# Moving SSM loads to ScalarE's queue, state products beside output products, and the slots of the attention around the query norms

## The chip, the cores and the metric

The kernel runs on one core of a Trainium2 chip. Five engines matter: TensorE (PE, with its weight loads as PEld), VectorE (DVE), ScalarE (ACT), GpSimd (POOL) and SyncE (SP). Each runs its own instructions in program order and waits for the others by semaphores. DMAs are issued by SP or ACT, as instructions in that engine's stream. The metric is the device time of one execution in microseconds; the times below are medians of several executions.

## The reference

One layer of a hybrid decoder for 256 prompt tokens and 8 x 4 decode tokens, 288 columns in all, width 2048, in fp32:

```
x = x + 1/2 SwiGLU_1(rmsnorm(x))
u, q, k, v = split(rmsnorm(x) @ w_in)          # 1024 + 1024 + 256 + 256 columns
y_ssm  = S5(u): h_t = lam_bar * h_(t-1) + B_bar u_t (complex), y = gelu(Re(C h) + D u), then a GLU
y_attn = sliding window attention over 128 keys, 16 query heads on 4 key heads,
         q and k normed per head, ALiBi, one sink per head
x = x + concat(rmsnorm(y_ssm), rmsnorm(y_attn)) @ w_out
x = x + 1/2 SwiGLU_2(rmsnorm(x))
```

The key and value caches and the SSM states are outputs too. The S5 part has 64 groups of 16 channels with 64 complex states; the kernel treats it in 8 blocks j of 128 channels, with the scan over chunks of 4 tokens (T=4), so that the steps within a chunk are small matrix products with prepared matrices (ma into the state, mb out of it) and the steps between chunks a scan with a decay (d0) in a rotating frame (rot).

## The kernel before, in words

All weights stream through in 677 pieces of at most 128 x 1024 fp32. Every fp32 product is three products of rounded parts (mm3, lines L290, L291, L292: high x high, low x high, high x low). For each piece SP loads the raw tile (L116), ACT casts the high part wh (L124), VectorE subtracts the low part wl (L125), and TensorE makes 24 matmuls with it. Class Weights sets the order: `W.next()` begins a **slot**, one for each piece. It first splits the piece two slots ahead, issues the raw loads ahead, then runs the actions that were registered for this slot with `W.at(slot, f)`, and only then the slot's own 24 matmuls follow. `W.spread(slot, generator)` runs one step of a generator in each slot from there on. Nothing else sets the order: it is a list written out by hand, and each engine keeps it.

The mixer's slots are counted here from `base`: 0 and 1 key, 2 to 17 the eight SSM blocks (two slots each), 18 and 19 key, 20 to 23 value, 24 to 39 the eight query tiles i (two heads each; two tiles, a pair m, share one run of norms), 40 to 71 w_out.

An SSM block j starts from s = 7, 9, ... (base + 2j + 5). Its projection is stored to scratch memory (ssm_u_store, L761, ACT's queue) and read back in another layout as U, four DMAs (ssm_u_load, L767, SP's queue). ssm_load_a and ssm_load_r read ma and rot (L771, L775), ssm_load_b mb (L789), all on SP. ssm_state makes 32 small matmuls (L798) into a rotated sum (L804 to L807, VectorE), then one slot later the scan (L810 to L814), then cs (L818 on ACT, L820 on POOL, L821), then L823, L824 and ACT's copy fin (L825). ssm_out makes 48 matmuls from U, cs and mb (L833) and a gelu (L837). For every two blocks, ssm_y_store writes the result out in four DMAs (L843, ACT's queue), ssm_y_load reads it back as yn (L847, SP's queue), and ssm_glu multiplies it with the GLU weights (L856, L861) and splits it for w_out (L743). ssm_norm is the chain of an rsqrt over 288 columns (L230 to L246) that gives R_ssm, with which the w_out results are scaled (L1177).

In the attention, q_square squares a query tile (L1007, ACT, reading qn of L1171), sums adds the squares over each head (L1025, TensorE) and starts row_rsqrt, a chain of one VectorE instruction (L970) and twelve small ones on POOL (L973 to L976). scores makes the logits on TensorE (L1043), scales them with the query norm (L1049, ACT) and adds the bias (L1053, VectorE), and runs the softmax, whose last step (L1001) multiplies the probabilities lg by the inverse sum. probs_t transposes them (L1062, TensorE; L1063) and pv multiplies with the values (L1075). The decode tokens have their own path (sample).

The helpers `get` and `put` are a DMA issued by SP and by ACT. `tt`, `ts` and `stt` are VectorE's tensor_tensor, tensor_scalar and scalar_tensor_tensor.

Of the kernel before, what the change touches and what calls it, by code (L numbers as in the profile page):

```python
# [14 lines left out]
ALU = mybir.AluOpType  # L15
AX = mybir.AxisListType

P = 128
# [15 lines left out]
EPS = 1e-6  # L34
# [656 lines left out]
def mix(tc, nc, io, es, W, base, e):  # L691
    act, dve, pool_e, pe = nc.scalar, nc.vector, nc.gpsimd, nc.tensor
    tt, ts, stt = dve.tensor_tensor, dve.tensor_scalar, dve.scalar_tensor_tensor
    x, R, gains, ident, acc = e["x"], e["R"], e["gains"], e["ident"], e["acc"]
    tp, dr, pm, pa = (e[k] for k in ("tp", "dr", "pm", "pa"))
    proj, mm3 = e["proj"], e["mm3"]
    put, get = act.dma_start, nc.sync.dma_start
# [16 lines left out]
    R_ssm = mp.tile([P, N], F32, name="R_ssm")  # L714
# [7 lines left out]
    yd = [dr.tile([2 * P, N], F32, name="yd%d" % j) for j in range(4)]  # L722
# [27 lines left out]
    MA, MB, ROT, D0, U, CS, UE, YG, YN, GL = ({} for _ in range(10))  # L750
# [12 lines left out]
    def ssm_u_load(j):  # L763
        U[j] = sm.tile([P, 4, W1], F32, name="U", bufs=4)
        src = ud[j].rearrange("(q c) (j t) -> j c q t", q=4, j=T)
        for jr in range(T):
            get(U[j][32 * jr:32 * jr + 32], src[jr])  # L767

    def ssm_load_a(j):
        MA[j] = sa.tile([P, 2, 4, P], F32, name="ma", bufs=2)  # L770
# [20 lines left out]
    def ssm_state(j):  # L791
        ma, u, rot = MA.pop(j), U[j], ROT.pop(j)
        b = []
        for i in range(2):
            ps = aux()
            for q in range(4):
                for hh in HALVES:
                    pe.matmul(ps[hh, q * W1:(q + 1) * W1], ma[:, i, q, hh], u[:, q], start=True, stop=True)  # L798
            b.append(ps[:, :N].rearrange("p (q t) -> p q t", q=4))
        br, bi = b[0][:, :, NB:], b[1][:, :, NB:]  # L800
        co, si = rot[:, :, 0, :], rot[:, :, 1, :]
        z, w = (sa.tile([P, 2, 4, NCH], F32, name="r" + n, bufs=2) for n in "zw")
        q = slice(4 * j, 4 * j + 4)
        tt(z[:, 1], br, co, op=ALU.mult)  # L804
        tt(w[:, 1], bi, si, op=ALU.mult)
        tt(z[:, 0], bi, co, op=ALU.mult)
        tt(w[:, 0], br, si, op=ALU.mult)  # L807
        yield
        for i in range(2):
            tt(fin_s[:, i, q, :], b[i][:, :, :NB], fin_s[:, i, q, :], op=ALU.add)  # L810
        tt(z[:, 1], z[:, 1], w[:, 1], op=ALU.add)
        tt(z[:, 0], z[:, 0], w[:, 0], op=ALU.subtract)
        for i in range(2):
            dve.tensor_tensor_scan(flat(w[:, i]), flat(D0[j % 2]), flat(z[:, i]), 0.0, op0=ALU.mult, op1=ALU.add)  # L814
        yield
        cs = CS[j % 2]
        for i in range(2):
            act.copy(cs[:, i, :, :NB], e["h0"][:, 1 - i, q, :])  # L818
        both = [P, 2, 4, NCH]
        pool_e.tensor_tensor(z, w, si[:, None].to_broadcast(both), op=ALU.mult)  # L820
        tt(cs[:, :, :, NB + 1:], w, co[:, None].to_broadcast(both), op=ALU.mult)  # L821
        yield
        tt(cs[:, 1, :, NB + 1:], cs[:, 1, :, NB + 1:], z[:, 0], op=ALU.subtract)  # L823
        tt(cs[:, 0, :, NB + 1:], cs[:, 0, :, NB + 1:], z[:, 1], op=ALU.add)  # L824
        act.copy(fin[:, :, q], cs[:, :, :, W1])  # L825

    def ssm_out(j):
# [16 lines left out]

    def ssm_y_load(j):
        YN[j] = sm.tile([P, 2, N], F32, name="yn", bufs=2)
        get(YN[j], yd[j].rearrange("(a p) n -> p a n", a=2))  # L847

    def glu_load():
        GL[0] = sm.tile([P, 8, P], F32, name="gl")  # L850
# [2 lines left out]
    def ssm_glu(j):  # L853
        yn = YN[j // 2][:, j % 2]
        ps = aux()
        pe.matmul(ps[:, :N], GL[0][:, j], yn, start=True, stop=True)  # L856
        t = tp.tile([P, N], F32, name="s1")
        act.activation(t, ps[:, :N], AF.Tanh, scale=0.5)
        yield
        y2 = tp.tile([P, N], F32, name="s2")  # L860
        stt(y2, t, 1.0, yn, op0=ALU.add, op1=ALU.mult)  # L861
        yield
        yield from y_split(ys, y2, 48 + j, j == 0, dve if j == 7 else pool_e)
# [16 lines left out]
    for j in range(8):  # L880
        s = base + 2 * j + 5
        W.at(s, ssm_u_store, j)
        W.at(s + 1 if j > 1 else base + 1 + j, ssm_load_a, j)
        W.at(s + 1 if j > 1 else base + 2 + j, ssm_load_r, j)
        W.at(s + 2, ssm_u_load, j)
        W.at(s + 2, ssm_decay, j)
        W.spread(s + 4, ssm_state(j), True)
        W.at(s + 6, ssm_load_b, j)
        W.at(s + 9, ssm_out, j)
        if j % 2:  # L890
            W.at(s + 10, ssm_y_store, j // 2)
            W.at(s + 11, ssm_y_load, j // 2)
            W.spread(s + 13, ssm_glu(j - 1))
            W.spread(s + 14, ssm_glu(j))
    W.at(s + 8, state_done)
    W.at(s + 17, ssm_done)

    def ssm_norm():
        for n, _ in enumerate(e["norm"](e["ones"], acc, R_ssm, 1.0 / 1024, 4 * EPS)):
            if n % 2:  # L900
                yield

    W.spread(s + 19, ssm_norm())

    def tok(ap, blk):

# [73 lines left out]
    def softmax(lg, parts, sink, w):  # L980

        m = mp.tile([P, w], F32, name="sm_m", bufs=4)
        es_ = mp.tile([P, w], F32, name="sm_e", bufs=4)
        l = mp.tile([P, w], F32, name="sm_l", bufs=4)
        for a, (lo, hi) in enumerate(parts):
            dve.tensor_reduce(m[:, 2 * a:2 * a + 2], lg[:, :, lo:hi], axis=AX.X, op=ALU.max)
        tt(m, m, sink, op=ALU.max)
        tt(es_, sink, m, op=ALU.subtract)
        ts(m, m, -1.0, None, op0=ALU.mult)
        yield  # L990
        for a, (lo, hi) in enumerate(parts):
            for hb in range(2):
                c = 2 * a + hb
                act.activation(lg[:, hb, lo:hi], lg[:, hb, lo:hi], AF.Exp, bias=m[:, c:c + 1],  # L994
                               accum_out=l[:, c:c + 1])
        act.activation(es_, es_, AF.Exp)
        yield
        tt(l, l, es_, op=ALU.add)
        dve.reciprocal(l, l)
        for a, (lo, hi) in enumerate(parts):  # L1000
            pool_e.tensor_tensor(lg[:, :, lo:hi], lg[:, :, lo:hi],  # L1001
                                 l[:, 2 * a:2 * a + 2, None].to_broadcast([P, 2, hi - lo]), op=ALU.mult)

    def q_square(i):
        qb = QN[i]
# [11 lines left out]
    def sums(m):  # L1017

        ps = aux()
        cols = 8  # L1020
        for i in (2 * m, 2 * m + 1):
            for blk in range(2):
                c = 4 * (i % 2) + 2 * blk
                for hh in HALVES:
                    pe.matmul(ps[hh, c:c + 2], QN[i][1][:, 128 * blk:128 * blk + 128][:, hh],  # L1025
                              bones[:, 0:128:64], start=True, stop=True)
        if m % 2:
            cols = 10
            for hh in HALVES:
                pe.matmul(ps[hh, 8:10], QS[m // 2][1][:, hh], bones[:, 0:128:64], start=True, stop=True)  # L1030
        v = mp.tile([P, 10], F32, name="rq_v", bufs=2)[:, :cols]
        ts(v, ps[:, :cols], 1.0 / 64, EPS, op0=ALU.mult, op1=ALU.add)
        RQ[m] = row_rsqrt(v, cols)

    def scores(i):
        p, g = divmod(i, 4)
        qb, sq = QN.pop(i)
        rq = RQ[i // 2][:, 4 * (i % 2):4 * (i % 2) + 4]
        pss = [aux() for _ in range(2)]
        for a, (bq, bk) in enumerate(((0, 0), (1, 0), (1, 1))):  # L1040
            for hb in range(2):
                pp = slice(64 * hb, 64 * hb + 64)
                pe.matmul(pss[hb][:, 128 * a:128 * a + 128], qb[pp, 128 * bq:128 * bq + 128],  # L1043
                          tok(kG[pp, p], bk), start=True, stop=True)
        yield
        lg = L[i] = late["a"].tile([P, 2, 384], F32, name="lg", bufs=3)
        for hb in range(2):
            for blk, (lo, hi) in enumerate(((0, 128), (128, 384))):
                act.activation(lg[:, hb, lo:hi], pss[hb][:, lo:hi], AF.Copy,  # L1049
                               scale=rq[:, 2 * blk + hb:2 * blk + hb + 1])  # L1050
        yield
        for hb in range(2):
            stt(lg[:, hb], dist, -SLOPES[heads_of(i)[hb]], lg[:, hb], op0=ALU.mult, op1=ALU.add)  # L1053
        yield from softmax(lg, ((0, 128), (128, 384)), sinkp[:, 4 * i:4 * i + 4], 4)
# [92 lines left out]
                next(y, None)  # L1147
            yield

    S = [base + 2 * (12 + i) + 2 for i in range(8)]  # L1150
    for i, s in enumerate(S):
        W.at(s, q_square, i)
        W.at(s + 11, pv, i)
    for m in range(4):
        W.at(S[2 * m + 1] + 1, sums, m)
    for i in range(8):
        W.spread(S[i | 1] + 1 + i % 2, scores(i))
    for i, s in enumerate(S):
        W.at(s + 9, probs_t, i)
    for p in range(2):  # L1160
        s = base + 2 * (12 + 4 * p + 3) + 2
        W.at(s - 4, cache_k_load, p)
# [190 lines left out]
```

## Time and profile before

| what | value |
|---|---|
| median of 3 runs | 1874.78 us (1873.18 to 1879.98) |
| profiled execution | 1878.1 us, span 1876.2 us, mean granted clock 0.996 |
| TensorE weight loads, share of the span | 98% |
| weights and all else moved by DMA | 359.08 MB, mean 191 GB/s |
| DMA share in the mixer's SSM stage (800 to 850 us) | 0.87 |
| DMA share in the attention stage (950 to 1000 us) | 0.35 |

The mixer runs from about 800 to 1100 us of the span; before and behind it lie the two feed-forward parts. A wait is put down to the engine or DMA whose semaphore came last by the profile. The granted clock of TensorE (PEclk) is a share of its full speed. A DMA's time to landing counts from its issue to the arrival of its data.

### The profile page before, as it was taken

What the parts mean: (1) busy time and instruction counts of PE and PEld (TensorE: products, weight loads), DVE (VectorE), ACT (ScalarE), POOL (GpSimd) and SP (SyncE); (2) the same over time, 40 slices, a digit from 0 to 9 for tenths busy, and PEclk for the clock granted to TensorE, in tenths of its full rate; (3) what the DMA queues carried; (4) which work ended last, traced back from release to release, by engine and by line L of the source; (5) the groups of instructions that cost most, each with busy time, mean ns of one, the idle gap of its engine ahead of it and who ended that gap; (6) DMA issues with size and microseconds to landing.
All of it is one profiled execution on the core that took longest, in us unless ns stands there. A gap on an engine that the chain in (4) does not pass through costs nothing.

```text
span 1876.2 us, 38183 instructions
## 1 busy us (share of the span) xinstructions
PE 1857.0 (99%) x15620; PEld 1839.1 (98%) x15620; DVE 1207.7 (64%) x1857; ACT 853.6 (45%) x1347; POOL 269.0 (14%) x342
## 2 busy tenths in 40 slices
PE   9999999999999999999989999999999999999999
PEld 9999999999999999998988999999999999999999
DVE  6677667666667755688887885555555555555554
ACT  6443444444444444643566554433444334434433
POOL 3201011000100100212236640000000000000000
PEclk9999999999999999999999999999999999999999
DMA  7555656556655764788733455556555565556555
GB/s 277 197 181 163 219 181 214 190 166 230 212 192 162 232 213 147 238 293 292 232 120 135 157 176 185 179 161 188 187 179 168 174 196 180 163 169 207 180 161 160
DMA packets 122624, 359.08 MB, mean 191 GB/s; under 512 B 22064, under 2 KB 30256, under 8 KB 121264
## 3 DMA queue, kind: packets, MB, share of 16 engines
q1 hardware_dynamic: 114496, 340.48, 56.7%
q10 hardware_dynamic: 7952, 16.16, 2.5%
q8 instruction: 122, 2.00, 0.4%
q14 instruction: 54, 0.44, 0.1%
HBM read 338.40 MB, written 20.22 MB: 191 GB/s over the span
## 4 chain that ended last, share of the span: by engine, by line
PE 93%; DVE 3%; ACT 1%; DMA 1%; POOL 1%; issue 1%; SPq 0%; ACTq 0%; POOLq 0%; DVEq 0%
PE main L290 30%; PE main L292 30%; PE main L291 30%; DVE wl L125 1%; ACT wh L124 1%; PE main L833 1%; DMA ud<-t 0%; PE main L798 0%; PE main L623 0%; PE main L629 0%; ACT lg L994 0%; DMA ma<-mats 0%; DMA raw<-in_w_gu 0%; POOL x L1178 0%; POOL lg L1001 0%
## 5 line engine op out<-in xcount | busy, mean ns | idle before, releaser
L125 DVE TENSOR_TENSOR wl<-raw,wh 128x1024 fp32r<-128x1024 f32 (+2 forms) x677 | 754.1, 1114 | 445.0 <-ACT wh L124 443.1
L290 PE MATMUL main<-xh,wh 128*128 128x288 f32 x3136 | 904.9, 289 | 0.5 <-ACT xh L216 0.5
L292 PE MATMUL main<-xh,wl 128*128 128x288 f32 x3136 | 899.7, 287 | 0.7 <-DVE wl L125 0.6
L291 PE MATMUL main<-xl,wh 128*128 128x288 f32 x3136 | 899.4, 287 | 0.1
L124 ACT CAST wh<-raw 128x1024 fp32r<-128x1024 f32 (+2 forms) x677 | 637.9, 944 | 495.9 <-PE main L291 335.4
L290 PEld LDWEIGHTS main<-xh,wh 128*128 128x128 f32 x3136 | 594.6, 190 | 3.9 <-ACT xh L216 0.8
L292 PEld LDWEIGHTS main<-xh,wl 128*128 128x128 f32 x3136 | 594.5, 190 | 1.7 <-DVE wl L125 0.8
L291 PEld LDWEIGHTS main<-xl,wh 128*128 128x128 f32 x3136 | 594.7, 190 | 1.3 <-DVE xl L217 0.8
L290 PE MATMUL main<-hh,wh 128*128 128x288 f32 x1664 | 478.2, 287 | 0.3 <-ACT s L1079 0.3
L291 PE MATMUL main<-hl,wh 128*128 128x288 f32 x1664 | 476.3, 286 | 0.6 <-DVE hl L743 0.6
L292 PE MATMUL main<-hh,wl 128*128 128x288 f32 x1664 | 476.2, 286 | 0.0
L290 PEld LDWEIGHTS main<-hh,wh 128*128 128x128 f32 x1664 | 314.8, 189 | 1.2 <-ACT s L1079 0.8
L291 PEld LDWEIGHTS main<-hl,wh 128*128 128x128 f32 x1664 | 314.8, 189 | 1.0 <-DVE hl L743 0.8
L292 PEld LDWEIGHTS main<-hh,wl 128*128 128x128 f32 x1664 | 314.8, 189 | 0.2 <-DVE wl L125 0.2
L364 POOL TENSOR_TENSOR s<-s,R 128x288 f32<-128x288 f32 x88 | 70.6, 803 | 1139.5 <-ACT s L363 1139.5
L373 ACT CAST hh<-h 128x288 fp32r<-128x288 f32 x88 | 38.1, 433 | 222.5 <-DVE h L372 222.5
L363 ACT ACTIVATE s<-t 128x288 f32<-128x288 f32 x88 | 39.1, 445 | 219.5 <-DVE t L362 219.5
L394 DVE SCALAR_TENSOR_TENSOR x<-main,x 128x288 f32<-128x288 f32 x128 | 58.4, 457 | 39.7 <-PE main L292 39.3
L372 DVE TENSOR_TENSOR h<-main,s 128x288 f32<-128x288 f32 x88 | 40.1, 456 | 55.5 <-PE main L292 55.2
L362 DVE TENSOR_TENSOR t<-main,R 128x288 f32<-128x288 f32 x88 | 40.2, 456 | 44.9 <-PE main L292 44.6
L374 DVE TENSOR_TENSOR hl<-h,hh 128x288 fp32r<-128x288 f32 x88 | 40.4, 459 | 44.0 <-ACT hh L373 44.0
L226 POOL TENSOR_TENSOR acc<-acc,sq 128x288 f32<-128x288 f32 x45 | 45.3, 1006 | 46.0 <-ACT sq L222 45.1
(262 smaller groups left out, 835.8 us busy)
## 6 DMA issues: line engine op xcount, KB each, us to landing
raw<-in_w_gu SPq DMA_DIRECT2D x349, 512.0 KB, 4.1
raw<-in_w_dn SPq DMA_DIRECT2D x128, 384.0 KB, 3.2
raw<-in_w_dn SPq DMA_DIRECT2D x128, 320.0 KB, 3.2
raw<-in_w_in SPq DMA_DIRECT2D x40, 512.0 KB, 4.9
raw<-in_w_out SPq DMA_DIRECT2D x32, 512.0 KB, 3.5
mats<-stage ACTq DMA_DIRECT2D x8, 1536.0 KB, 7.1
mb<-mats SPq DMA_DIRECT2D x8, 768.0 KB, 8.2
ma<-mats SPq DMA_DIRECT2D x8, 512.0 KB, 5.4
```

The source lines that it names most:

```text
L124: self.nc.scalar.copy(wh[:, :n], t[:, :n])
L125: self.nc.vector.tensor_tensor(wl[:, :n], t[:, :n], wh[:, :n].bitcast(F32), op=ALU.subtract)
L226: eng.tensor_tensor(acc, acc, sq, op=ALU.add)
L290: pe.matmul(ps, wh[:, s], woven(rh[k]), start=first and a == 0, stop=False)
L291: pe.matmul(ps, wh[:, s], woven(rl[k]), start=False, stop=False)
L292: pe.matmul(ps, wl[:, s], woven(rh[k]), start=False, stop=last and a == n - 1)
L362: dve.tensor_tensor(t1, pg[:, :N], R, op=ALU.mult)
L363: act.activation(s1, t1, AF.Silu)
L364: pool_e.tensor_tensor(s2, s1, R, op=ALU.mult)
L372: dve.tensor_tensor(halved(h), evens(pu[:, :N]), evens(s2), op=ALU.mult)
L374: dve.tensor_tensor(hl, h, hh.bitcast(F32), op=ALU.subtract)
L394: dve.scalar_tensor_tensor(x[d], ps[:, :N], 0.5, x[d], op0=ALU.mult, op1=ALU.add)
```

## The change

In the SSM part, U is loaded in slot s+1 instead of s+2 and by ACT instead of SP; ma and rot in slot s instead of s+1 (both for j over 1 in the latter case); the state products run in slot s+3 instead of s+4 for j over 1, which is the slot of ssm_out(j-3); the copy fin comes one slot after L823 and L824; yn is loaded by ACT; both GLU blocks of a pair start in slot s+13; the SSM norm starts a slot earlier and makes one step a slot instead of two.

In the attention, the softmax's last step is four VectorE instructions (L997 of the new file) instead of two on POOL; sums keeps its slots and the norm chain is split from it and put at the end of the same slot; scores, probs_t and pv get new slots, the first scores of each pair one slot later than before.

```diff
--- before.py
+++ after.py
@@ -764,7 +764,7 @@
         U[j] = sm.tile([P, 4, W1], F32, name="U", bufs=4)
         src = ud[j].rearrange("(q c) (j t) -> j c q t", q=4, j=T)
         for jr in range(T):
-            get(U[j][32 * jr:32 * jr + 32], src[jr])
+            put(U[j][32 * jr:32 * jr + 32], src[jr])
 
     def ssm_load_a(j):
         MA[j] = sa.tile([P, 2, 4, P], F32, name="ma", bufs=2)
@@ -822,6 +822,7 @@
         yield
         tt(cs[:, 1, :, NB + 1:], cs[:, 1, :, NB + 1:], z[:, 0], op=ALU.subtract)
         tt(cs[:, 0, :, NB + 1:], cs[:, 0, :, NB + 1:], z[:, 1], op=ALU.add)
+        yield
         act.copy(fin[:, :, q], cs[:, :, :, W1])
 
     def ssm_out(j):
@@ -844,7 +845,7 @@
 
     def ssm_y_load(j):
         YN[j] = sm.tile([P, 2, N], F32, name="yn", bufs=2)
-        get(YN[j], yd[j].rearrange("(a p) n -> p a n", a=2))
+        put(YN[j], yd[j].rearrange("(a p) n -> p a n", a=2))
 
     def glu_load():
         GL[0] = sm.tile([P, 8, P], F32, name="gl")
@@ -880,27 +881,21 @@
     for j in range(8):
         s = base + 2 * j + 5
         W.at(s, ssm_u_store, j)
-        W.at(s + 1 if j > 1 else base + 1 + j, ssm_load_a, j)
-        W.at(s + 1 if j > 1 else base + 2 + j, ssm_load_r, j)
-        W.at(s + 2, ssm_u_load, j)
+        W.at(s + 1, ssm_u_load, j)
+        W.at(s if j > 1 else base + 1 + j, ssm_load_a, j)
+        W.at(s if j > 1 else base + 2 + j, ssm_load_r, j)
         W.at(s + 2, ssm_decay, j)
-        W.spread(s + 4, ssm_state(j), True)
+        W.spread(s + (3 if j > 1 else 4), ssm_state(j), True)
         W.at(s + 6, ssm_load_b, j)
         W.at(s + 9, ssm_out, j)
         if j % 2:
             W.at(s + 10, ssm_y_store, j // 2)
             W.at(s + 11, ssm_y_load, j // 2)
             W.spread(s + 13, ssm_glu(j - 1))
-            W.spread(s + 14, ssm_glu(j))
+            W.spread(s + 13, ssm_glu(j))
     W.at(s + 8, state_done)
     W.at(s + 17, ssm_done)
-
-    def ssm_norm():
-        for n, _ in enumerate(e["norm"](e["ones"], acc, R_ssm, 1.0 / 1024, 4 * EPS)):
-            if n % 2:
-                yield
-
-    W.spread(s + 19, ssm_norm())
+    W.spread(s + 18, e["norm"](e["ones"], acc, R_ssm, 1.0 / 1024, 4 * EPS))
 
     def tok(ap, blk):
 
@@ -998,8 +993,8 @@
         tt(l, l, es_, op=ALU.add)
         dve.reciprocal(l, l)
         for a, (lo, hi) in enumerate(parts):
-            pool_e.tensor_tensor(lg[:, :, lo:hi], lg[:, :, lo:hi],
-                                 l[:, 2 * a:2 * a + 2, None].to_broadcast([P, 2, hi - lo]), op=ALU.mult)
+            for hb in range(2):
+                ts(lg[:, hb, lo:hi], lg[:, hb, lo:hi], l[:, 2 * a + hb:2 * a + hb + 1], None, op0=ALU.mult)
 
     def q_square(i):
         qb = QN[i]
@@ -1028,6 +1023,10 @@
             cols = 10
             for hh in HALVES:
                 pe.matmul(ps[hh, 8:10], QS[m // 2][1][:, hh], bones[:, 0:128:64], start=True, stop=True)
+        RQ[m] = ps, cols
+
+    def norms(m):
+        ps, cols = RQ[m]
         v = mp.tile([P, 10], F32, name="rq_v", bufs=2)[:, :cols]
         ts(v, ps[:, :cols], 1.0 / 64, EPS, op0=ALU.mult, op1=ALU.add)
         RQ[m] = row_rsqrt(v, cols)
@@ -1035,7 +1034,6 @@
     def scores(i):
         p, g = divmod(i, 4)
         qb, sq = QN.pop(i)
-        rq = RQ[i // 2][:, 4 * (i % 2):4 * (i % 2) + 4]
         pss = [aux() for _ in range(2)]
         for a, (bq, bk) in enumerate(((0, 0), (1, 0), (1, 1))):
             for hb in range(2):
@@ -1043,6 +1041,7 @@
                 pe.matmul(pss[hb][:, 128 * a:128 * a + 128], qb[pp, 128 * bq:128 * bq + 128],
                           tok(kG[pp, p], bk), start=True, stop=True)
         yield
+        rq = RQ[i // 2][:, 4 * (i % 2):4 * (i % 2) + 4]
         lg = L[i] = late["a"].tile([P, 2, 384], F32, name="lg", bufs=3)
         for hb in range(2):
             for blk, (lo, hi) in enumerate(((0, 128), (128, 384))):
@@ -1147,16 +1146,17 @@
                 next(y, None)
             yield
 
-    S = [base + 2 * (12 + i) + 2 for i in range(8)]
+    S = [base + 2 * (12 + (i | 1)) + 2 + i % 2 for i in range(8)]
     for i, s in enumerate(S):
-        W.at(s, q_square, i)
-        W.at(s + 11, pv, i)
+        W.at(base + 2 * (12 + i) + 2, q_square, i)
+        W.at(s + 10, pv, i)
     for m in range(4):
-        W.at(S[2 * m + 1] + 1, sums, m)
-    for i in range(8):
-        W.spread(S[i | 1] + 1 + i % 2, scores(i))
+        W.at(S[2 * m] + 1, sums, m)
+        W.at(S[2 * m] + 1, lambda m=m: W.at(W.slot, norms, m))
     for i, s in enumerate(S):
-        W.at(s + 9, probs_t, i)
+        W.spread(s + 2, scores(i))
+    for i, s in enumerate(S):
+        W.at(s + 8, probs_t, i)
     for p in range(2):
         s = base + 2 * (12 + 4 * p + 3) + 2
         W.at(s - 4, cache_k_load, p)
```

The order of ACT's instructions in slots 17 and 18, before (yd and ud are the scratch copies of the SSM's outputs and inputs; DMAHW0 to DMAHW7 are the completion semaphores that all DMAs of SP and ACT use in turn):

```order
L124 CAST wh_10968<-raw_10693 128x1024 [waits DMAHW4_49,PE_49,Activation_49]
L843 DMA yd0_10112<-yg_10790 32x8x72 [waits DMAHW5_49,Activation_49]
L843 DMA yd0_10112<-yg_10790 32x8x72 [waits DMAHW7_49]
L843 DMA yd0_10112<-yg_10790 32x8x72 [waits DMAHW2_49]
L843 DMA yd0_10112<-yg_10790 32x8x72 [waits DMAHW4_49]
L785 COPY d0_1_10165<-e4_137 128x4x63 [waits DVE_49]
L761 DMA ud6_10110<-t1_10896 128x288 [waits DMAHW6_49]
L818 COPY cs_1_10167<-h0_139 128x4x8 x2
L124 CAST wh_11042<-raw_10763 128x1024 [waits PE_49]
L837 ACTIVATE yg_11075<-main_11050 128x288 [waits PE_49]
L825 COPY fin_10099<-cs_1_10167 128x2x4 [waits DVE_49]
L124 CAST wh_11114<-raw_10833 128x1024 [waits PE_49]
```

And after, the same place:

```order
L124 CAST wh_11001<-raw_10721 128x1024 [waits PE_49,Activation_49]
L844 DMA yd0_10112<-yg_10800 32x8x72 [waits DMAHW6_49,Activation_49]
L844 DMA yd0_10112<-yg_10800 32x8x72 [waits DMAHW1_49]
L844 DMA yd0_10112<-yg_10800 32x8x72 [waits DMAHW3_49]
L844 DMA yd0_10112<-yg_10800 32x8x72 [waits DMAHW5_49]
L785 COPY d0_1_10165<-e4_137 128x4x63 [waits DVE_49]
L761 DMA ud6_10110<-t1_10908 128x288 [waits DMAHW7_49,DVE_49]
L124 CAST wh_11054<-raw_10773 128x1024 [waits PE_49]
L848 DMA yn_11060<-yd0_10112 128x2x288 [waits DMAHW5_49,DMAHW3_49,DMAHW6_49,DMAHW1_49,DMAHW0_49]
L838 ACTIVATE yg_11087<-main_11062 128x288 [waits PE_49]
L767 DMA U_11089<-ud6_10110 32x4x72 [waits DMAHW7_49]
L767 DMA U_11089<-ud6_10110 32x4x72 x2
```

The load of yn and those of U have come in between the weight casts (L124) and the gelu (L838, L837 before); the load of yn waits for five semaphores, and the first load of U for one.

The order of TensorE in slot 14, before, where the output products of block 0 stand between two weight pieces:

```order
L833 MATMUL main_10765<-U_10397,mb_10582 64x72 x2
L833 MATMUL main_10765<-cs_0_10163,mb_10582 64x72 x4
L833 MATMUL main_10765<-U_10397,mb_10582 64x72 x2
L833 MATMUL main_10765<-cs_0_10163,mb_10582 64x72 x4
L833 MATMUL main_10765<-U_10397,mb_10582 64x72 x2
L833 MATMUL main_10765<-cs_0_10163,mb_10582 64x72 x4
L290 MATMUL main_10758<-xh0_87,wh_10646 128x288
L291 MATMUL main_10758<-xl0_104,wh_10646 128x288
L292 MATMUL main_10758<-xh0_87,wl_10647 128x288
```

After, the same slot:

```order
L834 MATMUL main_10775<-U_10364,mb_10587 64x72 x2
L834 MATMUL main_10775<-cs_0_10163,mb_10587 64x72 x4
L834 MATMUL main_10775<-U_10364,mb_10587 64x72 x2
L834 MATMUL main_10775<-cs_0_10163,mb_10587 64x72 x4
L834 MATMUL main_10775<-U_10364,mb_10587 64x72 x2
L834 MATMUL main_10775<-cs_0_10163,mb_10587 64x72 x4
L798 MATMUL main_10813<-U_10656,ma_10591 64x72 x8
L798 MATMUL main_10822<-U_10656,ma_10591 64x72 x8
L290 MATMUL main_10768<-xh0_87,wh_10650 128x288
L291 MATMUL main_10768<-xl0_104,wh_10650 128x288
L292 MATMUL main_10768<-xh0_87,wl_10651 128x288
```

The state products of block 3 (L798), which came in the next slot before, now follow the output products (L834, which was L833) directly.

The order of POOL at the end of a norm chain (rq) of the attention, before; lg are probabilities, rq_a and rq_b norms for the decode tokens:

```order
L975 TENSOR_SCALAR rq_t<-rq_t 128x10 [waits Pool_49]
L976 TENSOR_TENSOR rq_o<-rq_t,rq_o 128x10 [waits Pool_49]
L1001 TENSOR_TENSOR lg<-lg,sm_l 128x2x128 [waits DVE_49,DMAHW7_49,PE_49,Activation_49]
L1001 TENSOR_TENSOR lg<-lg,sm_l 128x2x256 [waits Activation_49]
L1093 TENSOR_SCALAR rq_a<-rq_o,mcst 128x2 [waits Pool_49]
L1094 TENSOR_SCALAR rq_b<-rq_o,mcst 128x2
L1001 TENSOR_TENSOR lg<-lg,sm_l 128x2x128 [waits DVE_49,Activation_49]
L1001 TENSOR_TENSOR lg<-lg,sm_l 128x2x256 [waits Activation_49]
```

After, the same place:

```order
L970 TENSOR_SCALAR rq_t<-rq_t 128x10 [waits Pool_49]
L971 TENSOR_TENSOR rq_o<-rq_t,rq_o 128x10 [waits Pool_49]
L1092 TENSOR_SCALAR rq_a<-rq_o,mcst 128x2 [waits Pool_49]
L1093 TENSOR_SCALAR rq_b<-rq_o,mcst 128x2
L747 TENSOR_TENSOR acc<-acc,sq 128x288 [waits Activation_49]
```

The scalings of lg are gone from POOL, and the sum of squares for the norm (L747) follows the chain.

## The prediction

> **What bounds the kernel now.** I read the page first, for the share of each engine and the chain that ended last.
>
> ```profile
> PE 1857.0 (99%) x15620; PEld 1839.1 (98%) x15620; DVE 1207.7 (64%) x1857; ACT 853.6 (45%) x1347; POOL 269.0 (14%) x342
> PE 93%; DVE 3%; ACT 1%; DMA 1%; POOL 1%; issue 1%; SPq 0%; ACTq 0%; POOLq 0%; DVEq 0%
> ```
>
> TensorE is busy for 99% of the span and carries 93% of the chain. The change issues the same matmuls, so it can only win the time in which TensorE stands still or runs at a lower clock. The second view was the waits of TensorE (total, times, longest, in us); the third, TensorE in stretches of 50 us (busy time and count of PE, PEld, DVE, ACT, POOL, then granted clock, DMA share, GB/s).
>
> ```profile
> PE main L1062 <- POOL lg L1001: 3.7, 3, 2.2
> PE main L798 <- DMA U<-ud: 2.7, 1, 2.7
> PE main L1025 <- ACT qsq L1007: 2.1, 1, 2.1
> PE main L798 <- ACT cs L818: 2.0, 1, 2.0
> PE main L798 <- DVE rw L814: 1.4, 1, 1.4
> PE main L291 <- DVE hl L743: 0.6, 1, 0.6
> PE main L290 <- ACT s L1079: 0.3, 1, 0.3
> PE main L242 <- ACT h L934: 0.2, 1, 0.2
> ```
> ```profile
> 800.00:850.00 50.00, 49.81 (x498) 48.50 (x498) 43.70 (x75) 21.35 (x31) 8.75 (x10) 1.00 0.87 294
> 850.00:900.00 50.00, 43.98 (x577) 41.20 (x576) 42.75 (x83) 17.90 (x41) 10.09 (x6) 0.97 0.81 267
> 900.00:950.00 50.00, 49.38 (x530) 46.15 (x528) 39.37 (x83) 28.76 (x70) 13.70 (x30) 1.00 0.65 218
> 950.00:1000.00 50.00, 45.48 (x441) 40.54 (x442) 39.30 (x87) 35.29 (x107) 25.91 (x48) 0.90 0.35 117
> 1000.00:1050.00 50.00, 48.45 (x437) 46.55 (x436) 38.40 (x58) 29.74 (x72) 30.01 (x28) 1.00 0.44 149
> ```
>
> These eight waits are those of the mixer and sum to 13.0 us. To them comes clock: 0.03 x 50 = 1.5 us in 850 to 900 (SSM), 0.10 x 50 = 5.0 us in 950 to 1000 (attention). So 19.5 us is all there is to win.
>
> Who is really late at the three L798 waits? I went to the timeline (start, duration, engine; in brackets idle before it and releaser), and to the view of the tile U between 855 and 880.
>
> ```profile
> 861.61 5.89 ACTq L843 DMA_DIRECT2D yd<-yg  x4
> 867.54 0.40 ACT L785 COPY d<-e 128x252 f32<-128x252 f32 x1 [4.96 <-DVE rw L807]
> ```
> ```profile
> 865.54 6.24 SPq L767 DMA_DIRECT2D U<-ud  x4
> 876.57 3.81 SPq L767 DMA_DIRECT2D U<-ud  x4
> 894.59 1.75 SPq L767 DMA_DIRECT2D U<-ud  x4
> ```
> ```profile
> 875.37 1.28 PE L798 MATMUL main<-U,ma 128*64 128x72 f32 x32 [1.96 <-ACT cs L818]
> 898.05 1.16 PE L798 MATMUL main<-U,ma 128*64 128x72 f32 x30 [1.38 <-DVE rw L814]
> ```
> ```profile
> DMA to landing us min/median/max: 3.7/7.9/8.5
> ```
>
> The view names ACT and DVE for two of the three, but the four loads of U that start at 865.54 are issued until 865.54 + 6.24 = 871.78, and with the least landing time (3.7) from there that is 875.4, where the state products begin (875.37). Likewise 894.59 + 1.75 = 896.34 leaves 1.7 us to 898.05. All three waits, 6.1 us, are thus U loads that came late; that the names are wrong is my reading, not a row. The same rows show why: one small load does not take 1.5 us to issue by itself. SP stood still between the four, and so did ACT between its four yd stores (5.89, with 4.96 idle ahead of the next copy). In the order of the program each of these DMAs waits on a completion semaphore that an earlier DMA, eight issues back over both queues, must raise first. So a DMA on ACT can stop ACT until an old weight or matrix load has landed.
>
> **The SSM part.** The U loads move to ACT and one slot earlier, the matrices ma and rot one slot earlier, the state products (from j=2) one slot earlier, yn to ACT. Issue to landing of those transfers (KB each, median us):
>
> ```profile
> raw<-in_w_in SPq DMA_DIRECT2D x40, 512.0 KB, 4.9
> mb<-mats SPq DMA_DIRECT2D x8, 768.0 KB, 8.2
> ma<-mats SPq DMA_DIRECT2D x8, 512.0 KB, 5.4
> rot<-mats SPq DMA_DIRECT2D x8, 256.0 KB, 6.0
> ud<-t ACTq DMA_DIRECT2D x8, 144.0 KB, 4.6
> U<-ud SPq DMA_DIRECT2D x32, 36.0 KB, 5.7
> yd<-yg ACTq DMA_DIRECT2D x16, 72.0 KB, 3.8
> yn<-yd SPq DMA_DIRECT2D x4, 288.0 KB, 3.9
> ```
>
> What goes: the lead of U over its products stays two slots, but U now starts in the slot after ma, rot and mb (1536 KB together) and no longer directly behind them. I take the three waits as gone: -6.1, and the clock with them, -1.5.
>
> What comes, place by place. (1) Slot 12 is the first early state and U(2) is loaded in slot 10, after a slot without state or output products, so with the shortest lead; its loads wait for ma and rot of slot 9 (5.4 and 6.0). Between nothing and half of the 7.9 that a U load took here, 0 to 4; I take 1. (2) Slot 20: the GLU needs yn, whose load on ACT waits for the landing of its four stores (3.8), and behind it on ACT stand the gelu, the four U loads and the weight cast wh that TensorE needs two slots on. Nearest row: the four yd stores held ACT 5.89. Range 0 to 6; I take 2, because the cast has two slots of cover. (3) The other yn loads, slots 24 and 32, together 0.5 (0 to 3). (4) A wait of 2 us costs a dip of the clock here; half of the 1.5 to 2 that one costs, 1.0 (0 to 2). That gives back 4.5; the sum is -7.6 + 4.5 = -3.1, kept as -3. The bounds: -8 with all of it gained, +5 with waits (1) and (2) near their upper ends and one dip.
>
> VectorE in 800 to 900 (43.70 and 42.75 of 50) gets no work more; the fin copy a slot later takes a wait out of ACT:
>
> ```profile
> ACT fin L825 <- DVE cs L824: 16.4, 8, 3.4
> ```
>
> That was idle time beside TensorE; I cost it at nothing: it is the room in which ACT can wait for its DMAs instead, 2 us for each j, and if the DMAs wait longer than that it is gone.
>
> **The attention part.** Normalising the softmax goes from POOL, where it stood behind the chain of query norms, to VectorE, and the norms get a slot between their sums and the scores that use them. Groups by shape between 920 and 1052 (busy us, mean ns | idle before), and the waits of ACT there:
>
> ```profile
> L1001 POOL TENSOR_TENSOR lg<-lg,sm_l 128x512 f32<-128x512 f32 x8 | 9.6, 1196 | 0.0
> L1001 POOL TENSOR_TENSOR lg<-lg,sm_l 128x256 f32<-128x256 f32 x8 | 7.2, 905 | 4.2 <-DVE sm_l L999 2.4 <-ACT wh L124 1.8
> L1053 DVE SCALAR_TENSOR_TENSOR lg<-mcst,lg 128x384 f32<-128x384 f32 x16 | 8.7, 586 | 0.0
> L989 DVE TENSOR_SCALAR sm_m<-sm_m 128x4 f32<-128x4 f32 x8 | 1.4, 170 | 0.3
> ```
> ```profile
> ACT lg L1049 <- POOL rq_o L976: 5.7, 3, 2.9
> ```
> ```profile
> 950.00:960.00 10.00, 7.93 (x52) 6.43 (x53) 5.12 (x9) 5.89 (x16) 6.11 (x11) 0.66 0.61 209
> 980.00:990.00 10.00, 7.55 (x75) 6.63 (x74) 9.62 (x26) 6.57 (x25) 2.61 (x3) 0.83 0.16 52
> ```
>
> The POOL wait goes: -3.7. The clock of 0.66 right behind its longest wait is 0.34 x 10 = -3.4. On VectorE come four scalings per head pair; one lies between 170 ns (four elements) and 586 (384 elements), for 128 and 256 columns I estimate 0.2 and 0.4, so 1.2 us for a pair instead of 2.1 on POOL. Eight pairs are some 10 us over the 130 us of the stage, in which VectorE is busy 39.4, 39.3 and 38.4 of 50: hidden, except where it is full. That is 980 to 990 (9.62 of 10), the place of the qsq wait of 2.1: ACT waited there for VectorE's qn, which stood behind the SSM norm's two steps a slot and a softmax. The SSM norm now goes one step a slot and starts one slot earlier, and the sums of the last queries keep their slot, 41. That thins the queue by half and the scalings fill it again by 1.2, so I keep 1.2 of the 2.1 (0 to 2.5): -0.9. Its dip, 0.17 x 10 = 1.7, is kept at 0.4, since a wait of 1.2 shows no dip in these rows (the 1.38 at 898 and the 1.0 at POOL, in 1000 to 1050, show 1.00): -1.3. The three small waits (0.6, 0.3, 0.2) stay. Sum -3.7 - 3.4 - 0.9 - 1.3 = -9.3, bounds -11 and -5.
>
> **Sum.** -3.1 - 9.3 = -12.4. The profiled execution took 1878.1 us (span 1876.2, 1.9 outside it), which is 3.3 over the median of the runs, 1874.8. So 1865.7 for it, and 1862.4 for the median; I say 1862.5. For the chances, a measurement of this kernel can tell 0.5%, 9.4 us, from no change.
>
> [...] The clock fell after waits of 2.0 to 2.2 us, and not after the one of 2.7 (the 850 to 900 row has 1.5 us of loss in all, and it lies after 876). [...] As a rival (the same waits go, no dip ever was: 1874.8 - 7.2 = 1867.6) it gets 0.02, counted in A. [...]
>
> **Rivals.** *A, no measurable change (0.31).* The SSM gain is eaten by waits (1) to (3), and the qsq wait with its dip stays because the scalings sit where VectorE is full; what is left is the POOL term, 3.7 + 3.4, less some 0.6: -6.5, 1868.3. For it: 9.62 of 10 at 980, and 5.89 for four DMAs on ACT. Against it: the SSM norm leaves that place. It is also the result if U, with the same two slots of lead, comes as late as before. *B, slower (0.11).* ACT's in-order stream becomes the bound: at each of the six even slots 12 to 22 the U loads stand behind mb, ma or rot (8.2, 5.4, 6.0 to land), the state products now stand beside the output products in the same slot with nothing behind which to hide, and each comes 4 us late (the 5.89 row, less the 2 us of fin's room): 6 x 4 = 24, with six dips at 1.7, 10, so 34, less the 7.6 removed and 9.3 of attention: +17, 1892. It breaks even at 1.1 us a slot, 6 x (1.1 + 1.7) = 16.8 against 16.9, and is measurably slower from 2.7 us a slot. For it: rows of 5.89 and 6.24; against it: the loads come in a slot without ma and mb. *C, full recovery (0.13, within my forecast's side).* All 19.5 us are won: 1874.8 - 19.5 = 1855.3.
>
> **How the numbers follow.** Forecast 0.45, C 0.13, A 0.31, B 0.11. Low end 1855.0 is C; the upper end must take in A's upper part (SSM at +5 and attention at -5 is 1874.8) and leaves out B and a little of A: 1876.0. Faster by over 0.5% means under 1865.4: 0.45 + 0.13 = 0.58; same 0.31; slower 0.11.
>
> **What would show it.** Right: no TensorE wait for the scaled logits, the L798 waits below 2 us together, clock 1.00 in 950 to 960, U issued on ACT in under 3 us for four. Wrong: TensorE waits of 2 us or more at the state products of slots 12 to 22, at the GLU of slot 20, or at a weight piece for wh behind a DMA on ACT (A, B); a wait for qsq of 2 us with a dip behind (A); new VectorE waits at the transposes of the softmax.

## The result and the profile after

The changed kernel takes 1886.04 us (median of 5; before 1874.78): the ratio is 1.005, interval 1.0036 to 1.0064. So it is slower by about 9 us (7 to 12 by the interval; the two medians alone lie 11.3 apart), where 12 us faster were forecast. The profiled execution has a span of 1884.2 us against 1876.2, 8.0 more.

The waits of TensorE after:

```profile
PE main L798 <- DMA U<-ud: 6.5, 3, 3.2
PE main L857 <- DMA yn<-yd: 4.8, 2, 2.5
PE main L1020 <- ACT qsq L1002: 4.0, 2, 2.2
PE main L1061 <- DVE lg L997: 1.2, 1, 1.2
PE main L291 <- DVE hl L743: 0.6, 1, 0.6
PE main L1120 <- ACT pt L1062: 0.2, 1, 0.2
PE main L242 <- ACT h L929: 0.2, 1, 0.2
```

They sum to 17.5 us; before it was 13.0. The POOL wait is gone, as forecast. The U wait is as large as before (6.5 against 6.1), and two kinds are new: the GLU waits for yn (L857), and qsq is waited for twice instead of once. The same stretches as before:

```profile
800.00:850.00 50.00, 46.26 (x422) 45.02 (x422) 40.60 (x74) 17.02 (x24) 6.87 (x10) 0.97 0.85 284
850.00:900.00 50.00, 44.62 (x621) 41.85 (x621) 37.08 (x77) 16.71 (x38) 5.18 (x5) 0.97 0.87 278
900.00:950.00 50.00, 45.28 (x455) 42.32 (x450) 32.54 (x63) 22.27 (x50) 12.17 (x22) 0.93 0.64 193
950.00:1000.00 50.00, 47.99 (x455) 44.10 (x454) 44.69 (x117) 38.38 (x114) 12.87 (x28) 0.97 0.39 131
1000.00:1050.00 50.00, 48.41 (x479) 44.97 (x478) 39.79 (x83) 32.64 (x91) 25.02 (x31) 1.00 0.40 128
```

The clock lost 0.03 + 0.03 + 0.07 + 0.03 = 0.16 x 50 = 8.0 us, before 6.5. It goes in dips: each time the granted clock stands at half (0.50) for 3.41 us, which costs 1.7 (after, from 844.68, 885.64, 909.53, 936.84 and 991.45; before, from 876.39 and 985.62, and for twice as long from 951.49). Summed by dip that is 8.5 and 6.8, a little above the sums of the rounded shares. Longer waits (+4.5) and the clock (+1.5) make 6.0 of the 8.0; the mixer also starts 0.26 later, and what is left was not taken apart further. By the first weight matmul of each slot in the two traces, counted from the mixer's start, the changed kernel is behind by 5.1 us at slot 15, 3.9 at slot 23, 8.1 at slot 25 and 11.3 at slot 30; the attention then gives 6 us back by slot 37 and loses 2.9 by slot 52, where 8.1 is left.

**The first step, slot 12.** By the code s is 2j + 5, so block 0 starts at slot 5 and block 2 at slot 9; its U is now loaded in slot 10 and used in slot 12. ACT's timeline after (start, duration, engine; in brackets idle before and releaser):

```profile
823.16 2.78 ACTq L767 DMA_DIRECT2D U<-ud  x4
826.06 1.05 ACT L124 CAST wh<-raw 128x1024 fp32r<-128x1024 f32 x1 [4.63 <-DMA U<-ud]
829.69 1.91 ACTq L767 DMA_DIRECT2D U<-ud  x4
831.77 0.34 ACTq L761 DMA_DIRECT2D ud<-t  x1
837.05 2.52 ACTq L767 DMA_DIRECT2D U<-ud  x4
```

and before, on ACT and on SP:

```profile
828.94 0.38 ACTq L761 DMA_DIRECT2D ud<-t  x1
```
```profile
834.38 4.24 SPq L767 DMA_DIRECT2D U<-ud  x4
```

The loads of one U must wait until the store of its ud has landed, and ACT waits for that in its own stream (ud of block 2 took 5.2 us to land from 831.77, and its loads start at 837.05); the next store ud stands behind them. So ud(2) left at 831.77 instead of 828.94, and the loads of U(2) ran from 837.05 to 839.57, where SP before had issued them from 834.38 to 838.62. Written a slot earlier, they were issued later. The state products of block 2 were now due a slot earlier as well, and waited:

```profile
844.36 1.94 PE L798 MATMUL main<-U,ma 128*64 128x72 f32 x32 [3.23 <-DMA U<-ud]
```

At slot 16 (block 4, a wait of 3.0) it is not the same sequence. Its store left ACT at 850.35, 4.0 later than before (846.37), with TensorE 5 to 6 us behind by then; it landed in 3.5 us, and the four loads went out from 855.03 to 857.28 but took 8.0 to 9.7 us to land, where the median of this trace is 5.6. Why they landed so late was not taken apart.

The chain that ended last can be followed back to 857.87, and from there it runs through the stores and loads that ACT issues (pieces in order, many left out): 7.01 us for the store ud of block 5 to land, 7.43 for its last load of U, then the next store, and in the end the load of yn for which TensorE waits at slot 24.

```profile
859.57 7.01 DMA ud<-t
867.97 7.43 DMA U<-ud
875.81 7.33 DMA ud<-t
893.67 5.00 DMA raw<-in_w_in
898.69 0.31 ACTq L844
905.86 2.93 DMA yn<-yd
908.92 1.68 PE main L857 x4
```

No piece of this chain between 857.87 and 908.92 is TensorE's. Before, TensorE carried most of the same stretch, from 875.37 on.

**Slots 20 and 24.** The load of yn waits for the four stores yd, and these too stand in ACT's stream, where each waits for the completion semaphore of an older DMA: in the chain above the third of them leaves ACT at 898.69, when a weight piece issued at 893.67 has landed (5.00). After, for the second pair:

```profile
893.91 5.72 ACTq L844 DMA_DIRECT2D yd<-yg  x4
899.68 0.40 ACT L785 COPY d<-e 128x252 f32<-128x252 f32 x1 [4.74 <-DMA yd<-yg]
905.86 0.39 ACTq L848 DMA_DIRECT2D yn<-yd  x1
```

Before, the first of these four stores left at 887.29 and the other three took 1.59, and SP issued the load at 896.90:

```profile
887.29 0.33 ACTq L843 DMA_DIRECT2D yd<-yg  x1
887.65 1.59 ACTq L843 DMA_DIRECT2D yd<-yg  x3
```
```profile
896.90 0.39 SPq L847 DMA_DIRECT2D yn<-yd  x1
```

TensorE ran 5.3 us behind the kernel before at slot 21; the first store left 6.6 later than before and the load 9.0 later (905.86 - 896.90). TensorE waited 2.5 for it, and 2.3 for the first pair at slot 20.

**Slot 28.** ACT stood between the two tanh of a GLU pair:

```profile
928.03 0.65 ACTq L923 DMA_DIRECT2D out_kT<-s  x1
929.68 0.40 ACT L859 ACTIVATE s<-main 128x288 f32<-128x288 f32 x1
935.10 0.41 ACT L859 ACTIVATE s<-main 128x288 f32<-128x288 f32 x1 [5.02 <-DMA out_kT<-s]
```
```profile
936.17 0.40 PE L1020 MATMUL main<-mcst,qsq 128*64 128x2 f32 x8 [2.22 <-ACT qsq L1002]
```

The tanh's result (s) has two buffers, and one of them held the key rows that out_kT was storing (both are named s1 in the code). Before, the second tanh came a slot later and found the buffer free. Now ACT waited for the store's landing, the square qsq behind it came late, and TensorE waited 2.22 us at slot 29.

### The profile page after: what moved, and what is told of

Its sections match the earlier page's. It is cut to its first block, busy times and chain, and to the rows that moved or that the text cites. A ratio compares the mean times of both kernels' runs of the same rounds, so it can differ in the third digit from the quotient of the medians.

```text
span 1884.2 us, 38198 instructions
## 1 busy us (share of the span) xinstructions
PE 1859.5 (99%) x15620; PEld 1841.7 (98%) x15620; DVE 1207.0 (64%) x1893; ACT 850.1 (45%) x1347; POOL 249.9 (13%) x324
## 4 chain that ended last, share of the span: by engine, by line
PE 47%; DMA 2%; DVE 2%; ACT 2%; issue 1%; POOL 0%; ACTq 0%; DVEq 0%; POOLq 0%
PE main L290 15%; PE main L291 15%; PE main L292 15%; DMA ud<-t 1%; ACT wh L124 1%; DVE wl L125 0%; DMA U<-ud 0%; DMA out_kT<-s 0%; DMA raw<-in_w_in 0%; PE main L834 0%; ACT lg L1048 0%; POOL x L1178 0%; DVE sm_m L981 0%; PE main L1041 0%; POOL acc L747 0%
## 5 line engine op out<-in xcount | busy, mean ns | idle before, releaser
L124 ACT CAST wh<-raw 128x1024 fp32r<-128x1024 f32 (+2 forms) x677 | 637.2, 943 | 500.9 <-PE main L291 332.9
L1178 POOL TENSOR_TENSOR x<-x,t 128x288 f32<-128x288 f32 x32 | 47.7, 1495 | 41.8 <-DVE t L1177 41.0
```

The source lines that it names most:

```text
L124: self.nc.scalar.copy(wh[:, :n], t[:, :n])
L1178: eng.tensor_tensor(x[d], x[d], t, op=ALU.add)
```

## The experiments

Three theories stood against each other: the loads on ACT do the harm (1), the earlier slots do (2), or the attention part does (3). All ratios are to the kernel before, with the interval behind them.

**Each half alone.** First the attention part and the SSM norm's new slots, with the SSM part as before:

```diff
-            put(U[j][32 * jr:32 * jr + 32], src[jr])
+            get(U[j][32 * jr:32 * jr + 32], src[jr])
...
-        W.spread(s + (3 if j > 1 else 4), ssm_state(j), True)
+        W.spread(s + 4, ssm_state(j), True)
```

(and likewise yn, the slots of U, ma, rot, the second GLU and the extra yield of the fin copy).

> The attention part alone (softmax scaling on VectorE, norms split from sums, new slots, SSM norm one step a slot), with the SSM part as before. If the SSM part carries the loss (theory 1, the loads on ACT, or theory 2, the earlier slots): the POOL wait 3.7 and its 3.4 of clock go, the qsq wait at slot 29 (2.2 and 1.7 of clock) does not appear, some 2 to 3 us of waits and more changes of work stay: 3 to 7 us faster than before, 1868 to 1872. If the attention part carries it (theory 3): no faster than before, 1875 or more.

Measured: 0.9984 (0.9975 to 0.9993), 1874.08 us: by the ratio 3 us faster, the low end of the first expectation; the time itself lies between the two ranges. Its profile has a wait that neither kernel shows:

```profile
PE main L242 <- DVE acc L747: 3.1, 1, 3.1
```

The SSM norm, begun a slot earlier, meets the last sum of squares of a GLU that is still a slot later. Then the SSM part alone, the reverse edit on the kernel before (SSM norm as before):

> The SSM part alone, attention and SSM norm as before. Theories 1 and 2: the mixer loses 8 us up to slot 28 as in the changed kernel and then keeps the POOL wait: 8 to 12 us slower than before, 1883 to 1887. Theory 3: within 3 us of before.

Measured: 1.006 (1.0042 to 1.0078), 1888.44 us: by the ratio 11 us slower, as theories 1 and 2 had it. The loss lies in the SSM part; theory 3 falls. The two halves, 11 and -3, make 8 of the 9 us.

**Queue or slot.** The changed kernel with U and yn issued by SP again and every slot as changed:

```diff
-            put(U[j][32 * jr:32 * jr + 32], src[jr])
+            get(U[j][32 * jr:32 * jr + 32], src[jr])
...
-        put(YN[j], yd[j].rearrange("(a p) n -> p a n", a=2))
+        get(YN[j], yd[j].rearrange("(a p) n -> p a n", a=2))
```

> The changed kernel with the loads of U and yn on SP again, all slots new. Theory 1 (loads on ACT wait there for the landing of their own stores and hold up the casts and stores behind them): the waits at slots 12, 20 and 24 (3.2, 2.3, 2.5 and three dips of 1.7) go for the most part, 8 to 14 us faster than the changed kernel, 1872 to 1878. Theory 2 (the slot is too early whatever the queue): within 3 us of the changed kernel.

Measured: 0.9985 (0.9976 to 0.9994), 1875.01 us, against 1.005: in these slots the queue is worth about 12 us, as theory 1 had it. But not every wait went:

```profile
PE main L1020 <- ACT qsq L1002: 6.4, 2, 4.7
PE main L857 <- DMA yn<-yd: 4.3, 2, 3.0
PE main L798 <- DMA U<-ud: 1.1, 2, 0.8
```

The U waits fell from 6.5 to 1.1, in the earlier slots; the waits for yn stayed and the one for qsq grew. Each such list is of one execution, and the waits differ from one to the next: this one took 1878.56, 3.6 us over the median of its runs.

**Which of the two loads.** Only U back on SP, and only yn back on SP (one line each of the diff above):

> The changed kernel with only the loads of U on SP, yn still on ACT. If it is U's four loads that hold up ACT (each must wait there for the landing of ud): nearly all of the 11 us that U and yn on SP gave back, 1875 to 1878. If it is yn, which waits on ACT for its stores: 1882 to 1886.

Measured: 1.0008 (0.9997 to 1.0019), 1878.83 us, a little outside the first range.

> The changed kernel with only yn's loads on SP, U still on ACT. If U carries the loss: 1882 to 1887. If yn does: 1875 to 1878. If each holds up the other, both lie between.

Measured: 1.0021 (1.0012 to 1.0029), 1881.19 us. From 1.005, U alone gives back 0.4% (8 us) and yn alone 0.3% (5 us); together 0.65% (12). Each carries a part, the third of the cases expected. With U on SP the U wait is small and yn's is not:

```profile
PE main L857 <- DMA yn<-yd: 6.4, 2, 3.7
PE main L798 <- DMA U<-ud: 1.2, 1, 1.2
```

With yn on SP it is the other way round, and no wait for yn is left:

```profile
PE main L798 <- DMA U<-ud: 7.5, 4, 2.5
```

**The queue by itself.** The kernel before with one line changed, slots as before:

```diff
-            get(U[j][32 * jr:32 * jr + 32], src[jr])
+            put(U[j][32 * jr:32 * jr + 32], src[jr])
```

> The kernel before with one line changed: the four loads of U issued by ACT, in the same slot, s+2. If the queue alone does the harm (ACT stands at those loads for older DMAs, and its casts and stores come late): 3 to 8 us slower than before. If a load costs the same from either queue and only the slot matters: within 2 us of before.

Measured: 1.0017 (1.0008 to 1.0025), 1879.54 us, 3 us slower, the low end of the first expectation: the harm is there without any new slot, but smaller than in the changed kernel, where the store and its load are only one slot apart and yn is on ACT too.

**The GLU pair and the shared buffer.** First the second GLU a slot later:

```diff
-            W.spread(s + 13, ssm_glu(j))
+            W.spread(s + 14, ssm_glu(j))
```

> The changed kernel with the second GLU block a slot later again (s+14). Theory: the second GLU's tanh shares its two buffers with the rows that out_kT still stores, so ACT stands 5.0 us in slot 28 and the sums at slot 29 come 2.2 late with a dip of 1.7. With it a slot later both go: 3 to 5 us faster than the changed kernel. Rival: ACT is late there from its yd and yn DMAs anyway: within 1 us of the changed kernel.

Measured: 1.0026 (1.0015 to 1.0037), 1882.14 us. No wait for qsq is left in its profile, but the wait for the last sum of squares (3.2) has come instead, as in the attention part alone. So this edit mixes two things. A cleaner one leaves every slot and gives the key rows another buffer:

```diff
-        kT = tp.tile([P, N], F32, name="s1")
+        kT = tp.tile([P, N], F32, name="h")
```

> The changed kernel with the key rows that out_kT stores in another buffer than the GLU's tanh, all slots and queues as changed. If ACT's 5.0 us in slot 28 come from that shared buffer: they go, and with them the wait for qsq at slot 29 (2.2) and its dip (1.7): 3 to 5 us faster than the changed kernel, 1881 to 1883. If ACT is late there from its own DMAs: within 1 us, 1885 to 1887.

Measured: 1.002 (1.0011 to 1.003), 1881.49 us, against 1.005, as the first expectation had it. In the profile both tanh follow each other without the 5.02 us between them:

```profile
930.87 0.70 ACT L859 ACTIVATE s<-main 128x288 f32<-128x288 f32 x2
```

**What the attention is worth.** The attention part with the SSM norm in its old slots:

```diff
-    W.spread(s + 18, e["norm"](e["ones"], acc, R_ssm, 1.0 / 1024, 4 * EPS))
+    W.spread(s + 19, ssm_norm())
```

> The attention part alone, with the SSM norm in its old slots (s+19, two steps a slot). With the norm moved, the attention part alone showed a new wait of 3.1 us for the last sum of squares at slot 37 and a dip of 1.7. If that is the norm's earlier slot meeting the unpaired GLU: both go, 4 to 6 us faster than with the norm moved, 1868 to 1871, and the waits for qsq at slot 41 come back in part (0 to 2). If the attention part is simply worth 2.5: 1873 to 1876.

Measured: 0.9978 (0.9968 to 0.9987), 1872.74 us: 4 us faster than before (2.4 to 6.0). Against the same part with the norm moved (0.9984) that is about 1 us and within the intervals, where 4 to 6 were expected: that expectation missed, and a cost of the norm's slot is not shown. The wait for the sum of squares is gone, but one for qsq at slot 41 has come in its place; what stays:

```profile
PE main L798 <- DMA U<-ud: 5.7, 3, 2.6
PE main L1025 <- ACT qsq L1007: 2.5, 1, 2.5
PE main L1066 <- DVE lg L1002: 1.2, 1, 1.2
```

**Putting it together.** Three kernels look for the rest: U and yn on SP with the GLU and the norm in their old slots (the edits shown for these, together), U and yn on SP with the key rows' own buffer, and the attention part with U one slot earlier on SP and the state products where they were (the last diff below, against before).

> The changed kernel with U and yn on SP, the second GLU a slot later and the SSM norm in its old slots. If the three causes (loads on ACT; the second GLU beside the first; the norm's slot) are all, the SSM slots and the attention's gains stay: 6 to 12 us faster than before, 1864 to 1870. If the early state products cost by themselves: no better than the attention part alone with the old norm, 0.998 of before or more.

Measured: 0.9978 (0.9969 to 0.9987), 1871.67 us: about 4 us, so the 6 to 12 did not come. It equals the attention part alone with the old norm (0.9978), from which it differs by the SSM slots: even with the loads on SP these slots gained nothing that can be measured.

> The changed kernel with U and yn on SP and the key rows in another buffer, all slots as changed. If queue (12 us) and shared buffer (5 us) add up: 5 to 9 us faster than before, ratio 0.995 to 0.997. If the yn wait at slots 20 and 24 stays as with U and yn on SP alone (4.3 and two dips), the ratio is 0.997 or more.

Measured: 0.9976 (0.9965 to 0.9986), 1871.3 us, the best of all, though not apart from the two at 0.9978, and short of the 5 to 9 us: the second expectation held. With the loads on SP the buffer is worth 0.1% (0.9985 to 0.9976, within the intervals), where it was worth 0.3% with them on ACT, so the two gains do not simply add up. The yn wait stayed:

```profile
PE main L857 <- DMA yn<-yd: 3.9, 1, 3.9
PE main L798 <- DMA U<-ud: 1.8, 2, 1.4
PE main L1020 <- ACT qsq L1002: 1.7, 1, 1.7
```

```diff
-        W.at(s + 2, ssm_u_load, j)
+        W.at(s + 1, ssm_u_load, j)
```

> The attention part with the old norm slots, and the U loads one slot earlier on SP, with the state products in their old slots, so with three slots of lead instead of two. If the U waits come from too short a lead: the 5.7 us of U waits of the attention part alone go to below 1.5 and the ratio to before is 0.994 to 0.996. If SP, standing for the landing of ud, makes the weight loads late instead: waits for wl or wh at weight pieces, ratio 0.998 or more.

Measured: 0.9982 (0.9973 to 0.9991), 1873.85 us. The U waits fell from 5.7 to 2.7, above the expected 1.5, and a wait for yn of 1.6 came; no weight piece waited more. So the ratio of the second case came, but not for its reason.

So every way of removing the U waits in the SSM slots ends about where the attention part ends without it. In the slots up to 20 the waits for U are exchanged for a wait for yn there, of 4.0 and 3.9 us in the first two of these kernels. In the second of them the trace shows what this wait hangs on: the last of the four stores yd was issued at about 870 and took 8.6 us to land (6.9 before), and SP issued the load of yn only then. The view of yd gives the landing, SP's timeline the load:

```profile
DMA to landing us min/median/max: 2.9/3.7/8.6
```
```profile
878.65 0.37 SPq L848 DMA_DIRECT2D yn<-yd  x1
```

Why that store took so long stays open. While it was under way, the DMA engines were busy for 0.63, 0.99 and 1.06 of the time in the three stretches of 3 us from 868 to 877; that this set the 8.6 is only argued.

## Why the prediction was wrong

**The three U waits taken as gone (-6.1).** This is the step that failed first. For blocks 5 and 7 they did go, to 0.1 at slot 18 and nothing at slot 22; block 4 still waited, 3.0 at slot 16, and block 2 was new with 3.2 at slot 12: 6.5 in all, with two small ones, in place of 6.1. (That all three waits before were for U, which the prediction argued against the names in its view, is borne out by the attention part with the norm in its old slots: its SSM part is that of before, and its view names U for all three, 5.7.) The prediction counted the lead from U's load to its products, two slots, and saw that it stayed. It did not count the lead from the store of ud to the load of U, which shrank from two slots to one. So the loads had to stand for the store's landing, and now on the engine that issues the next store; for block 4 that store was late by 4.0 and the landing of its loads slow as well. With U on SP, the same slots gave 1.1: for the U waits the slots were as good as forecast, the queue was not. The SSM gain of 3.1 still did not come on SP, where a wait for yn took the place of those for U.

**Place (1), slot 12: 1 us, bounds 0 to 4.** Measured 3.2 and a dip. The mechanism named (ma and rot of slot 9) was not the one that decided; it was the store ud of slot 9, issued at 831.77, 5.3 us ahead of the loads.

**Places (2) and (3), yn: 2 + 0.5.** Measured 2.3 + 2.5, and two dips where half a one was priced. "The cast has two slots of cover" held: TensorE never waited for a wh. What had no cover were ACT's own stores, whose landing the next loads need (up to 6.4 us for the second pair's yd, 7.01 and 7.33 for the two ud of the chain); the step named as queued behind the load the gelu, the U loads and the cast, and left out the stores.

**The GLU pair.** The prediction had no term for the second GLU's slot. It cost 2.2 us at slot 29 and a dip; the buffer alone changed the ratio by 0.3% (5.6 us).

**The attention, -9.3.** The direction was right and the size was not: -4 (2.4 to 6.0). The POOL wait went, 3.7. The qsq wait at slot 41 was kept at 1.2 with 0.4 for its dip; it measured 1.7 after and a whole dip, and 2.5 with the norm in its old slots: the square there still comes right behind VectorE's qn (after, it starts at 990.13, when the qn of 989.68 has taken its 0.42). The scalings were "hidden", but TensorE waited 1.2 for one of them at slot 48. The clock terms (-3.4 and -1.3) were read from one execution as if each went for good.

**The rivals.** B had the right sign and the right engine: ACT's stream in order became the bound. Its place and price were not right: not six state slots at 4 us each, +17, but two state slots, two GLU slots and slot 28, about +9. A was right in that waits (1) to (3) eat the SSM gain, but they ate more than the gain. The rival without any dip (1867.6) is the sum of 12.4 less its four clock terms, 5.2, which gives its 7.2; no run shows these two kernels so, and in their traces the clock cost 6.5 us before and 8.0 after.

**The queue itself.** A load of U took 5.7 us to land from SP before and 5.6 from ACT after:

```profile
U<-ud ACTq DMA_DIRECT2D x32, 36.0 KB, 5.6
```

In the same slots, with U on SP again, it took 3.9:

```profile
U<-ud SPq DMA_DIRECT2D x32, 36.0 KB, 3.9
```

So the transfer gained nothing from the other engine; but the wait ahead of the issue moved along with the load, and with it came a loss, 12 us by the run with both loads on SP.

## What to carry to other kernels

Before moving a DMA to an engine that computes, ask what the DMA itself must wait for, and treat that wait as an instruction of that engine: here what stood behind it in the stream was late by it, the next store above all (ud of block 2 left at 831.77 instead of 828.94). When a load is moved earlier, check the lead on both of its ends, to its consumer and from its producer. And two steps that are put into one slot need the buffers of both at the same time, also against a store that still reads one (5.02 us of ACT at slot 28).

## What the runs showed of the hardware

The clock's dip does not follow from a wait's length alone. The kernel before lost clock behind waits of 2.0, 2.1 and 2.2 us and not behind one of 2.7; the changed one behind waits of 3.2, 2.3, 2.5, 2.2 and 1.7, and not behind one of 3.0 at slot 16. In each of the two traces the dips of the mixer begin whole multiples of 3.41 us apart (before 22 and 10 of them, after 12, 7, 8 and 16). Laid out in such intervals, the traces show dips where TensorE stood still for long within one of them. Before, the wait of 2.7 fell on both sides of an edge between two, 1.16 and 1.52 us, and the interval behind it ran at full clock; the wait of 2.0 lay within one interval, and the next was halved (the number behind the length is TensorE's busy time, the third from the end the clock):

```profile
862.74:866.15 3.41, 1.89 (x38) 1.84 (x39) 3.41 (x4) 0.00 (x0) 2.12 (x1) 1.00 0.89 223
866.15:869.57 3.42, 3.42 (x53) 3.27 (x53) 1.69 (x5) 0.96 (x4) 0.00 (x0) 1.00 1.01 363
872.98:876.39 3.41, 1.45 (x36) 1.26 (x34) 3.38 (x5) 1.78 (x4) 1.85 (x1) 1.00 0.73 213
876.39:879.80 3.41, 3.41 (x20) 3.27 (x16) 2.25 (x5) 0.00 (x0) 0.37 (x1) 0.50 1.05 400
```

In these two traces, from 800 to 1060 us, all seven intervals at full clock with 1.74 us or more of standing still were followed by a halved one, of the four with 1.44 to 1.66 one was (1.66, from 982.21 before), and none with 1.26 or less. The 3.0 of slot 16 was split too, 1.51 and 1.44. The second half of the long dip, from 954.90 before, does not fit in: it follows an interval that was itself halved, with 0.58 of standing still. So here a wait of 2 to 3 us cost its 1.7 or not by where it fell on these intervals, which was read from the trace alone; a dip should be priced with a chance. Executions of one kernel differ in it: of 29 of the kernel before, the two with a mean clock of 1.000 took 1874.37 and 1873.34 us, the three with 0.995 took 1876.42 to 1879.38. So a profiled execution can differ from the median: the attention part with the old norm had waits of 2.6 and 2.5 us in its profile, and yet a clock of 1.00 in every stretch from 800 to 1050. Its span is 8.1 us shorter than before (1868.1 against 1876.2), and the ratio of the runs says 4.
